# A dense and mixture-of-experts trunk on one core: other places for the adaLN weight sums in the mixer and in the dense channel mixer

## The chip, the cores and the metric

The kernel runs on one core of a Trainium2 chip. The metric is the device time of one execution in microseconds (us), given as the median of several runs. One profiled execution is read with the hardware profiler; its engines are TensorE (PE), VectorE (DVE), ScalarE (ACT), GpSimd (POOL) and SyncE (SP), which here issues most DMAs.

## What is computed

Two layers over 512 tokens of width 1024. Each layer has six modulation vectors (adaLN), each of 1024 numbers, that are a product of one row, silu(c), with a matrix of 1024 x 6144; a norm and a mixer (gated linear attention and retention); and a norm and a channel mixer, dense in layer 0, with 8 experts in layer 1.

```python
def reference(x, c, positions, ada_w, ada_b, norm_mix_g, norm_ffn_g, w_in, ...):
    cond = jax.nn.silu(c)
    for layer in range(DEPTH):                      # DEPTH = 2
        mod = (cond @ ada_w[layer] + ada_b[layer])[:, None, :]
        sh1, sc1, g1, sh2, sc2, g2 = jnp.split(mod, 6, axis=-1)
        h = rms_norm(x, norm_mix_g[layer]) * (1.0 + sc1) + sh1
        x = x + g1 * hybrid_mixer(h, positions, w_in[layer], ...)
        h = rms_norm(x, norm_ffn_g[layer]) * (1.0 + sc2) + sh2
        if layer % 2 == 0:
            y = swiglu(h, ffn_w1[i], ffn_w3[i], ffn_w2[i])     # D_FF = 2816
        else:
            y = moe_swiglu(h, router_w[i], moe_w1[i], moe_w3[i], moe_w2[i])
        x = x + g2 * y
    return rms_norm(x, final_g)
```

## The kernel before

The residual stream stays on the chip as eight tiles xT of 128 channels x 512 tokens. Weights arrive in f32 by SP's DMAs and are split into a high and a low f16 half: ACT casts hi (L202), DVE subtracts lo (L203). Each product of the mixers is three matmuls (mm3, L220 to L222): high x high, low x high, high x low.

**The adaLN sums.** The first two vectors of layer 0 are needed at once and have a path of their own. All others go through a queue of 40 units (ada_queue), in the order 2, 4, 3, 5 of layer 0 and then 1, 0, 2, 4, 3, 5 of layer 1; a vector has two column blocks q of 512, and a block has two units h, one for each half of the 1024 rows. ada_load issues the two DMAs of a unit (ada, 512 KB each) on POOL's queue into four buffers, so two units are in flight. ada_use adds its four row blocks into acc on DVE, each times a column of silu(c): the first by L297, the others by L299. After the second unit of a pair ACT casts the sum (acch, L305), DVE subtracts (accl, L306), and ada_sum is put on a list: eight one-column products on PE (pm, L232) that add over the partitions, and the modulation's columns on DVE (mod, L235). The list is emptied by ada_finish at the next call.

ada_some(n, least) makes n steps; a step uses the oldest unit if two have been loaded, and loads the next. With least = LATER = 28 it stops when 28 units are left in the queue, so that 12 units, the layer-0 vectors, belong to the layer-0 mixer and 28 to the dense channel mixer. ada_rest uses what has been loaded. Steps stand in the mixer at the end of each 256 columns of a projection (project) and in every second token tile of the value projections (project_v, n = 1 and 2); ada_rest stands after the first column block of the output projection. In the dense channel mixer (dense_ffn) ada_some(2) stands at the end of each of the 11 iterations of the up loop, which take 256 of the 2816 columns each, and after each of the four column blocks of the second products (pd); ada_rest stands at the end.

**The norms.** Norm.feed squares each new piece of xT (sq, L365, ACT) and adds the squares (ssq, L367, DVE). PE adds over the partitions (pms, L372), DVE takes the mean (ms, L379), computes the reciprocal root in steps (L340 to L347) and makes a diagonal (dg, L390) that PE spreads to all partitions (prb, L391); then DVE and ACT make the normed input in two halves (u, hl on DVE L406, L413; hh on ACT L408 to L412). The last column block of the output projection and of the second products is done in two halves of 256 tokens, and so is the norm behind it. Norm f is the one ahead of the dense channel mixer, norm m the one ahead of the second mixer; there PE also transposes xT to token-major tiles (tt, L1116), which ACT copies out (xt, L1118), before the first products pf_k and pf_q.

**What sets the order.** A scheduler puts the instructions of each engine in an order at build time; each engine then works its queue strictly in that order. The first sum of a unit keeps its place in program order (keep_in_program_order), and the pm products come after a product named by last_mm (issue_after). What depends on the emission order, such as where ada_some is called, so moves the order of all engines around it.

Of the kernel before, what the change touches and what calls it, by code (L numbers as in the profile page):

```python
# [117 lines left out]
def trunk(ctx, tc, a, out):  # L118
# [346 lines left out]
    def mixer(l, hh, hl, ws, sp, ga_bank=None, tokens=None):  # L465
# [18 lines left out]
        def project_v(c0, name):  # L484

            ws = [wsplit(w_in[:, i * 4:i * 4 + 4, c0:c0 + 512], 4, 512, f"{name}{l}_{i}") for i in range(2)]
            vs = []
            for t in range(NT):
                pt = psum(f"pv_{name}{l}_{t}", "pj")
                s = slice(t * P, (t + 1) * P)  # L490
                for k in range(KC):
                    wh, wl = ws[k // 4]
                    mm3(pt, hh[k][:, s], hl[k][:, s], wh[k % 4], wl[k % 4], k == 0, k == KC - 1)
                v = tl(f"{name}{t}", tag="v", bufs=5)
                nc.scalar.mul(v, pt, SCL)
                vs.append(v)
                if t % 2:
                    ada_some(t // 2 + 1, LATER)
            return vs


# [288 lines left out]
        w_out = kview(a["w_out"][l])  # L790
        if tokens:
            return tokens(tl, w_out, oh, ol)
        norm = Norm(f"f{l}")
        for c in range(0, D, 256):
            wh, wl = wsplit(w_out[:, :, c:c + 256], KC, 256, f"wo{l}_{c}")
            for half in (None,) if c < D - 256 else range(2):
                s = slice(0, T) if half is None else HALF[half]
                for b in range(2):
                    pj = psum(f"po_{l}_{c}_{b}_{half}", "pj")[:, 0:s.stop - s.start]
                    for k in range(KC):  # L800
                        mm3(pj, wh[k][:, b * P:(b + 1) * P], wl[k][:, b * P:(b + 1) * P], oh[k][:, s],
                            ol[k][:, s], k == 0, k == KC - 1)
                    d = c // P + b
                    nc.vector.scalar_tensor_tensor(
                        xT[d][:, s], pj, mods[l, 2][:, d:d + 1], xT[d][:, s], op0=ALU.mult, op1=ALU.add)
                    norm.feed(d, half)
            if c == 0:
                ada_rest()
        return norm


    def dense_ffn(hh, hl, sp, after):
# [3 lines left out]
        for f in range(0, nf, 2):  # L816
# [9 lines left out]
            for half, b in [(h, b) for h in range(2) for b in range(2)] if f == 0 else [(None, 0), (None, 1)]:  # L826
                s = slice(0, T) if half is None else HALF[half]
                pp, g = [x[:, s] for x in pps[b]], gs[b][:, s]
                steps = [(j, k) for j in range(2) for k in range(KC)]
                if half is not None:  # L830
                    steps.sort(key=lambda x: x[1])
                for j, k in steps:
                    c = slice(b * P, (b + 1) * P)
                    wh, wl = ((w1h, w1l), (w3h, w3l))[j]
                    mm3(pp[j], wh[k][:, c], wl[k][:, c], hh[k][:, s], hl[k][:, s], k == 0, k == KC - 1)
                nc.scalar.activation(g, pp[0], AF.Silu, scale=SCL)
                nc.vector.scalar_tensor_tensor(g, pp[1], 1.0 / WS, g, op0=ALU.mult, op1=ALU.mult)
                hi, lo = ah[f + b][:, s], al[f + b][:, s]
                nc.scalar.copy(hi, g)
                nc.vector.tensor_tensor(lo, g, hi, op=ALU.subtract)  # L840
            with behind(after if f < 4 else ()):
                ada_some(2)
        norm = Norm("m1")
        for c in range(0, D, 256):
# [3 lines left out]
            for half in (None,) if c < D - 256 else range(2):  # L848
# [7 lines left out]
                for b in range(2):  # L856
# [1 line left out]
                    nc.vector.scalar_tensor_tensor(  # L858
                        xT[d][:, s], pd[b], mods[0, 5][:, d:d + 1], xT[d][:, s], op0=ALU.mult, op1=ALU.add)
                    norm.feed(d, half)  # L860
            ada_some(2)
        ada_rest()
        return norm


# [646 lines left out]
```

## Time and profile before

| | us |
|---|---|
| median of 3 runs | 1400.43 (1398.14 to 1401.98) |
| the profiled execution | 1400.13 |
| its span, first to last instruction | 1398.4 |
| PE busy | 1335.8 |
| DVE busy | 1009.0 |
| ACT busy | 684.0 |
| granted clock of PE, mean | 0.968 |

The stages in the profiled execution: the first norm and loads up to about 70 us, the first mixer to 246, its output projection to 289, the up products of the dense channel mixer from 297 to about 525, its second products to 646, the second mixer from 664 to about 880, then the experts. The span is some 1.7 us shorter than the time of the same execution. Bars of busy time add up what an engine does, not what it waits for; a bracket at the end of a row of a timeline is the idle time ahead of it and what ended that.

### The profile page before, as it was taken

Reading aid. Unit: us, or ns where it says so; the run is one execution under the profiler, and the core shown is the slowest. Engines: PE = TensorE matmul, PEld = TensorE weight load, DVE = VectorE, ACT = ScalarE, POOL = GpSimd, SP = SyncE. Lnnn points to the kernel's source line nnn. Section 1 sums busy time; section 2 is a strip of 40 time slices with the busy share of each in tenths; the row PEclk is TensorE's granted clock in tenths of the full one; section 3 lists DMA queues with packets and bytes.
Section 4 is the critical chain, followed back from the end, with each engine's and each line's share of the span. In section 5 each row is a group of like instructions: output and inputs, shape, how many; then the busy total and the mean of one; then the engine's idle time right before and its main releaser. Section 6 shows DMA issues by size and latency. Waiting matters only on the chain.

```text
span 1398.4 us, 28543 instructions
## 1 busy us (share of the span) xinstructions
PE 1335.8 (96%) x11801; PEld 944.8 (68%) x11801; DVE 1009.0 (72%) x1849; ACT 684.0 (49%) x1099; POOL 167.5 (12%) x177
## 2 busy tenths in 40 slices
PE   6899999989999999997999999999999999999985
PEld 5455556475444444466755555579999999999983
DVE  6867887784676565656456876798988888878683
ACT  4362233443333323223552333477877877877563
POOL 0020100010111110110200310500000000000552
PEclk7789999989999999998999999999999999999997
DMA  9862452334565665453411210089999999989841
GB/s 325 291 210 92 132 170 64 121 120 144 197 230 174 201 212 173 152 205 104 138 61 61 91 36 1 1 316 384 356 323 348 360 315 361 352 303 353 310 154 63
DMA packets 167614, 279.79 MB, mean 200 GB/s; under 512 B 6352, under 2 KB 90332, under 8 KB 167476
## 3 DMA queue, kind: packets, MB, share of 16 engines
q1 hardware_dynamic: 153396, 229.01, 48.2%
q0 software_dynamic: 13936, 48.61, 10.5%
q8 instruction: 94, 1.54, 0.4%
q10 hardware_dynamic: 144, 0.26, 0.1%
q14 instruction: 44, 0.36, 0.1%
HBM read 271.80 MB, written 6.06 MB: 199 GB/s over the span
## 4 chain that ended last, share of the span: by engine, by line
PE 81%; DVE 9%; DMA 4%; ACT 3%; issue 1%; SPq 1%; POOL 0%; DVEq 0%; ACTq 0%; POOLq 0%
PE u L220 6%; PE u L221 6%; PE u L222 5%; PE eu L1153 5%; PE eu L1155 5%; PE eu L1152 5%; PE ed L1155 3%; PE ed L1153 3%; PE ed L1152 3%; PE pg L1174 2%; PE pd_None L220 2%; PE pd_None L222 2%; PE pd_None L221 2%; PE pj_gate L220 2%; PE pj_gate L221 2%; PE pj_gate L222 2%
## 5 line engine op out<-in xcount | busy, mean ns | idle before, releaser
L222 PE MATMUL u<-hh_f,lo_w 128*128 128x512 f16 (+1 forms) x384 | 139.7, 365 | 0.0
L221 PE MATMUL u<-hl_f,hi_w 128*128 128x512 f16 (+1 forms) x384 | 139.7, 365 | 0.0
L220 PE MATMUL u<-hh_f,hi_w 128*128 128x512 f16 (+1 forms) x384 | 138.2, 366 | 0.0
L203 DVE SCALAR_TENSOR_TENSOR lo_w<-raw_w,hi_w 128x512 f16<-128x512 f32 (+1 forms) x136 | 84.8, 674 | 52.1 <-ACT hi_w L202 52.0
L285 POOL DMA_DIRECT2D ada<-in_ada_w x80 | 57.9, 723 | 480.0 <-DVE acc L299 461.4
L202 ACT ACTIVATE hi_w<-raw_w 128x512 f16<-128x512 f32 (+1 forms) x136 | 72.8, 604 | 82.9 <-PE u L221 63.1
L299 DVE SCALAR_TENSOR_TENSOR acc<-ada,conds,acc 128x512 f32<-128x512 f32 x140 | 105.1, 750 | 3.5 <-DMA ada<-in_ada_w 0.7
L222 PEld LDWEIGHTS <-lo_w 128*128 128x128 f16 x604 | 59.6, 99 | 55.5
L220 PEld LDWEIGHTS <-hi_w 128*128 128x128 f16 x604 | 59.7, 99 | 54.1
L221 PEld LDWEIGHTS <-hi_w 128*128 128x128 f16 x604 | 59.5, 99 | 54.1
L1342 POOL DMA_INDIRECT y<-ybuf,rows x16 | 26.1, 1628 | 395.5 <-DMA raw_e7moe_w<-in_moe_w 388.7
L222 PE MATMUL pd_None<-ah,lo_w 128*128 128x512 f16 x132 | 50.1, 380 | 0.0
L221 PE MATMUL pd_None<-al,hi_w 128*128 128x512 f16 x132 | 50.1, 379 | 0.0
L220 PE MATMUL pd_None<-ah,hi_w 128*128 128x512 f16 x132 | 50.1, 379 | 0.0
L305 ACT CAST acch<-acc 128x512 f16<-128x512 f32 x20 | 12.3, 616 | 76.7 <-DVE acc L299 76.7
L220 PE MATMUL pj_gate<-hh_m,hi_gate 128*128 128x512 f16 x128 | 48.6, 379 | 0.8 <-ACT g L743 0.8
L222 PE MATMUL pj_gate<-hh_m,lo_gate 128*128 128x512 f16 x128 | 48.6, 380 | 0.0
L221 PE MATMUL pj_gate<-hl_m,hi_gate 128*128 128x512 f16 x128 | 48.6, 379 | 0.0
L203 DVE SCALAR_TENSOR_TENSOR lo_e7moe_w<-raw_e7moe_w,hi_e7moe_w 128x2048 f16<-128x2048 f32 (+3 forms) x21 | 39.1, 1872 | 7.7 <-ACT hi_e7moe_w L202 4.8
L203 DVE SCALAR_TENSOR_TENSOR lo_e5moe_w<-raw_e5moe_w,hi_e5moe_w 128x2048 f16<-128x2048 f32 (+1 forms) x18 | 37.9, 2112 | 8.8 <-ACT hi_e5moe_w L202 8.7
L203 DVE SCALAR_TENSOR_TENSOR lo_e2moe_w<-raw_e2moe_w,hi_e2moe_w 128x2048 f16<-128x2048 f32 (+1 forms) x18 | 38.0, 2113 | 7.4 <-ACT hi_e2moe_w L202 7.1
L203 DVE SCALAR_TENSOR_TENSOR lo_e3moe_w<-raw_e3moe_w,hi_e3moe_w 128x2048 f16<-128x2048 f32 (+1 forms) x18 | 37.9, 2111 | 6.6 <-ACT hi_e3moe_w L202 6.5
(570 smaller groups left out, 4187.8 us busy)
## 6 DMA issues: line engine op xcount, KB each, us to landing
ada<-in_ada_w POOLq DMA_DIRECT2D x80, 512.0 KB, 5.2
raw_w<-in_ffn_w SPq DMA_DIRECT2D x26, 1024.0 KB
raw_e1moe_w<-in_moe_w SPq DMA_DIRECT2D x12, 1024.0 KB
raw_e2moe_w<-in_moe_w SPq DMA_DIRECT2D x12, 1024.0 KB
raw_e3moe_w<-in_moe_w SPq DMA_DIRECT2D x12, 1024.0 KB
raw_e4moe_w<-in_moe_w SPq DMA_DIRECT2D x12, 1024.0 KB
raw_e5moe_w<-in_moe_w SPq DMA_DIRECT2D x12, 1024.0 KB
raw_e6moe_w<-in_moe_w SPq DMA_DIRECT2D x12, 1024.0 KB
```

The source lines that it names most:

```text
L202: nc.scalar.mul(hi, raw, WS)
L203: nc.vector.scalar_tensor_tensor(lo, raw, WS, hi, op0=ALU.mult, op1=ALU.subtract)
L220: nc.tensor.matmul(dst, wh, xh, start=first, stop=False)
L221: nc.tensor.matmul(dst, wh, xl, start=False, stop=False)
L222: last_mm[:] = [nc.tensor.matmul(dst, wl, xh, start=False, stop=last)]
L285: nc.gpsimd.dma_start(r, view[:, k:k + 2])
L299: op = nc.vector.scalar_tensor_tensor(acc, x, c, acc, op0=ALU.mult, op1=ALU.add)
L1152: nc.tensor.matmul(dst, wh[:, s], x1, start=(first and i == 0), stop=False)
L1153: nc.tensor.matmul(dst, wh[:, s], x2, start=False, stop=False)
L1155: nc.tensor.matmul(dst, wl[:, s], x1, start=False, stop=(last and i == len(ws) - 1))
L1174: nc.tensor.matmul(pg[:, 0:W], ht[j][t][d // 4][:, d % 4 * P:(d % 4 + 1) * P], oneh[:, t], start=(t == 0), stop=(t == NT - 1))
L1342: nc.gpsimd.indirect_dma_start(out=y, out_offset=None, in_=ybuf[half], in_offset=bass.IndirectOffsetOnAxis(ap=rows[:, i, t:t + 1], axis=0))
```

## The change

Three places at which sums are made are moved. In the value projections one step is made in each of the four token tiles (4 in all, 3 before). ada_rest stands ahead of the output projection. In the up loop one more step stands between the two halves of an iteration from the third iteration on (f from 4 on, where the tokens are not halved), and during the second products only ada_rest is left, after the first column block.

```diff
@@ project_v
-                if t % 2:
-                    ada_some(t // 2 + 1, LATER)
+                ada_some(1, LATER)
             return vs
@@ the mixer, ahead of the output projection
+        ada_rest()
         norm = Norm(f"f{l}")
         for c in range(0, D, 256):
@@ the output projection, end of a column block
-            if c == 0:
-                ada_rest()
@@ dense_ffn, up loop, end of a half b
                 nc.vector.tensor_tensor(lo, g, hi, op=ALU.subtract)
+                if half is None and b == 0:
+                    ada_some(1)
             with behind(after if f < 4 else ()):
                 ada_some(2)
@@ dense_ffn, second products, end of a column block
-            ada_some(2)
-        ada_rest()
+            if c == 0:
+                ada_rest()
         return norm
```

The three places in the order of the instructions. First DVE's queue at the end of the output projection, before. Here po_768_1_1 is the last product (last column block, second column tile, second token half), acc_3_1 the last pair of sums of layer 0, and ms_f_0 the mean of the first token half:

```order
420 L299 SCALAR_TENSOR_TENSOR acc_3_1_2296<-ada_3_1_4_2204,conds,acc_3_1_2296 128x512
421 L367 TENSOR_TENSOR ssq_f_2339<-ssq_f_2339,sq_f_None 128x512
422 L804 SCALAR_TENSOR_TENSOR xT_103<-po_768_0_1_2621,mod_2_670,xT_103 128x256
423 L299 SCALAR_TENSOR_TENSOR acc_3_1_2296<-ada_3_1_4_2204,conds,acc_3_1_2296 128x512
424 L367 TENSOR_TENSOR ssq_f_2339<-ssq_f_2339,sq_f_0_2568 128x256
425 L299 SCALAR_TENSOR_TENSOR acc_3_1_2296<-ada_3_1_6_2206,conds,acc_3_1_2296 128x512
426 L804 SCALAR_TENSOR_TENSOR xT_104<-po_768_1_1_2652,mod_2_670,xT_104 128x256
427 L299 SCALAR_TENSOR_TENSOR acc_3_1_2296<-ada_3_1_6_2206,conds,acc_3_1_2296 128x512
428 L306 TENSOR_TENSOR accl_3_1_2377<-acc_3_1_2296,acch_3_1_2376 128x512
429 L379 TENSOR_SCALAR ms_f_0_2603<-pms_f_0_2340 128x2
```

The same place after:

```order
412 L804 SCALAR_TENSOR_TENSOR xT_103<-po_768_0_0_2542,mod_2_670,xT_103 128x256
413 L804 SCALAR_TENSOR_TENSOR xT_104<-po_768_1_0_2573,mod_2_670,xT_104 128x256
414 L367 TENSOR_TENSOR ssq_f_2357<-ssq_f_2357,sq_f_0_2568 128x256
415 L804 SCALAR_TENSOR_TENSOR xT_103<-po_768_0_1_2621,mod_2_670,xT_103 128x256
416 L379 TENSOR_SCALAR ms_f_0_2603<-pms_f_0_2358 128x2
417 L340 TENSOR_SCALAR ry_f_0_2605<-ms_f_0_2603 128x2
```

The sums are gone from there (they stand before the first xT update of the projection), and the mean of the first half stands ahead of the last xT update. On PE the products pms_f of that mean stand, before, behind the last product of the projection and behind the first pm product; this is PE's queue before:

```order
2216 L222 LDWEIGHTS lo_wo_768_2533
2217 L222 MATMUL po_768_1_1_2652<-oh_3_0_2282,lo_wo_768_2533 128x256
2218 L232 LDWEIGHTS acch_3_1_2376
2219 L232 MATMUL pm_3_512_2380<-one_90,acch_3_1_2376 128x1
2220 L372 MATMUL pms_f_0_2340<-cst,ssq_f_2339 128x1 x2
2221 L372 MATMUL pms_f_0_2340<-cst,sq_f_0_2599 128x1 x2
2222 L232 LDWEIGHTS accl_3_1_2377
2223 L232 MATMUL pm_3_512_2380<-one_90,accl_3_1_2377 128x1
```

In the new order pms_f_0 stands behind the sixth of the 24 matmuls of po_768_1_1, and no pm product stands between that and the first u product. Second, PE's queue behind the second products: before, the transposes of the sixth tile of tt are separated from the fifth by the eight pm products of the last pair of layer 1 and by prb_m, the spread of the second half's norm:

```order
6094 L1116 MATMUL tt_0_5918<-cst,xT_103 128x128
6095 L1116 MATMUL tt_0_5918<-cst,xT_104 128x128
6096 L372 MATMUL pms_m_1_4901<-cst,sq_m_1_5697 128x1 x2
6097 L232 LDWEIGHTS acch_5_1_5720
6098 L232 MATMUL pm_5_512_5724<-one_90,acch_5_1_5720 128x1
6099 L391 MATMUL prb_m_1_5809<-dg_m_1_5808,cst 128x128 x2
6100 L232 LDWEIGHTS accl_5_1_5721
6101 L232 MATMUL pm_5_512_5724<-one_90,accl_5_1_5721 128x1
```

After:

```order
6118 L1116 MATMUL tt_2_5932<-cst,xT_103 128x128
6119 L1116 MATMUL tt_2_5932<-cst,xT_104 128x128
6120 L372 MATMUL pms_m_1_5028<-cst,sq_m_1_5730 128x1 x2
6121 L1116 MATMUL tt_3_5939<-cst,xT_101 128x128
6122 L1116 MATMUL tt_3_5939<-cst,xT_102 128x128
6123 L1116 MATMUL tt_3_5939<-cst,xT_103 128x128
6124 L1116 MATMUL tt_3_5939<-cst,xT_104 128x128
6125 L220 LDWEIGHTS hi_first_0_5738
6126 L220 MATMUL pf_k_0_6007<-hh_m_5777,hi_first_0_5738 128x256
```

No pm product is left there, the first products follow the transposes, and prb_m_1 stands behind 32 of them. On ACT all eight xt copies now stand ahead of the third hh. Third, the up loop on PE, after; before, the eight pm products of a pair stand between the last product of an iteration and the first of the next:

```order
3040 L222 LDWEIGHTS lo_w_6_3406
3041 L222 MATMUL u_6_0_3430<-hh_f_2697,lo_w_6_3406 128x512
3042 L232 LDWEIGHTS acch_5_1_3312
3043 L232 MATMUL pm_5_512_3372<-one_90,acch_5_1_3312 128x1
3044 L220 LDWEIGHTS hi_w_6_3405
3045 L220 MATMUL u_6_0_3430<-hh_f_2722,hi_w_6_3405 128x512
```

They now stand inside the products of one u tile.

## Rows read from the trace of the kernel before

**Rows 1.** Page, part 1: busy us (share of span) of each engine.

```profile
PE 1335.8 (96%) x11801; PEld 944.8 (68%) x11801; DVE 1009.0 (72%) x1849; ACT 684.0 (49%) x1099; POOL 167.5 (12%) x177
```

**Rows 2.** Busy time by stretches, columns as in the first line.

```profile
core 0: us, PE busy (x) PEld busy (x) DVE busy (x) ACT busy (x) POOL busy (x), PEclk, DMA share, GB/s
100.00:180.00 80.00, 80.00 (x434) 44.16 (x434) 63.89 (x161) 24.84 (x56) 4.44 (x7) 0.97 0.40 124
...
300.00:400.00 100.00, 100.00 (x563) 54.50 (x562) 62.65 (x110) 39.80 (x80) 12.56 (x17) 0.98 0.48 158
400.00:500.00 100.00, 100.00 (x500) 45.86 (x499) 67.97 (x110) 34.92 (x64) 14.46 (x20) 1.00 0.61 198
...
700.00:760.00 60.00, 60.00 (x328) 33.63 (x326) 39.17 (x98) 23.76 (x43) 0.00 (x0) 1.00 0.23 71
```

**Rows 3.** DVE, end of output projection: start, duration (us), engine, line, operation.

```profile
285.70 0.49 DVE L804 SCALAR_TENSOR_TENSOR xT<-po,mod,xT 128x256 f32<-128x256 f32 x1
...
288.41 0.43 DVE L367 TENSOR_TENSOR ssq_f<-ssq_f,sq_f 128x256 f32<-128x256 f32 x1
...
292.41 0.16 DVE L379 TENSOR_SCALAR ms_f<-pms_f 128x2 f32<-128x2 f32 x1 [0.44 <-PE pms_f L372]
...
294.22 0.48 DVE L390 TENSOR_SCALAR dg_f<-cst,ry_f 128x128 f32<-128x128 f32 x2
```

**Rows 4.** Timeline of PE, end of the output projection.

```profile
289.14 0.27 PE L222 MATMUL po<-oh,lo_wo 128*128 128x256 f16 x1
291.30 0.18 PE L232 MATMUL pm<-one,acch 128*128 128x1 f16 x1 [1.89 <-ACT acch L305]
291.34 0.58 PE L372 MATMUL pms_f<-cst,ssq_f 128*128 128x1 f32 x4
...
294.65 1.19 PE L391 MATMUL prb_f<-dg_f,cst 128*128 128x128 f32 x4 [2.11 <-DVE dg_f L390]
...
297.20 1.01 PE L220 MATMUL u<-hh_f,hi_w 128*128 128x256 f16 x4
```

**Rows 5.** Timeline of DVE behind the second products.

```profile
648.24 1.29 DVE L203 SCALAR_TENSOR_TENSOR lo_gv<-raw_gv,hi_gv 128x512 f16<-128x512 f32 x2
649.45 1.26 DVE L406 SCALAR_TENSOR_TENSOR u_m<-xT,A1m,prb_m 128x256 f32<-128x256 f32 x3
...
651.22 0.75 DVE L299 SCALAR_TENSOR_TENSOR acc<-ada,conds,acc 128x512 f32<-128x512 f32 x1
...
657.63 0.75 DVE L299 SCALAR_TENSOR_TENSOR acc<-ada,conds,acc 128x512 f32<-128x512 f32 x1
...
658.88 0.48 DVE L390 TENSOR_SCALAR dg_m<-cst,ry_m 128x128 f32<-128x128 f32 x2
```

**Rows 6.** Timeline of ACT behind the second products.

```profile
644.31 4.48 ACT L202 ACTIVATE hi_gv<-raw_gv 128x512 f16<-128x512 f32 x8 [1.15 <-PE pd L221]
...
660.99 1.55 ACT L1118 COPY xt<-tt 128x512 f32<-128x512 f32 x3
```

**Rows 7.** Timeline of PE behind the second products.

```profile
659.08 0.18 PE L232 MATMUL pm<-one,acch 128*128 128x1 f16 x1 [9.28 <-ACT acch L305]
...
664.44 0.42 PE L220 MATMUL pf_k<-hh_m,hi_first 128*128 128x256 f16 x1
```

**Rows 8.** Busy time by stretches around both places, columns as above.

```profile
292.00:296.00 4.00, 1.89 (x18) 1.83 (x17) 2.46 (x14) 0.00 (x0) 0.00 (x0) 0.60 0.57 194
296.00:300.00 4.00, 4.00 (x21) 3.19 (x21) 3.72 (x15) 1.76 (x4) 0.66 (x1) 0.50 0.00 0
660.00:664.00 4.00, 3.05 (x21) 2.84 (x20) 2.96 (x12) 3.62 (x9) 0.00 (x0) 0.50 0.00 0
```

**Rows 9.** Page, part 5 (L285, L299), and landing time of ada loads.

```profile
L285 POOL DMA_DIRECT2D ada<-in_ada_w x80 | 57.9, 723 | 480.0 <-DVE acc L299 461.4
...
L299 DVE SCALAR_TENSOR_TENSOR acc<-ada,conds,acc 128x512 f32<-128x512 f32 x140 | 105.1, 750 | 3.5 <-DMA ada<-in_ada_w 0.7
...
DMA to landing us min/median/max: 4.0/5.2/7.8
```

## The prediction

> **What bounds the kernel now.** First the busy line of the page: TensorE (PE) is busy for 1335.8 of 1398.4 us, so the time can only fall where PE stands still or where its clock is down [rows 1]. Then the busy time by stretches. In the mixer from 100 to 180 us and in the up products of the dense channel mixer from 300 to 500 us PE is busy all the time, VectorE (DVE) for 63 to 80% of it, and the DMA engines carry up to 198 GB/s [rows 2]. In such a stretch DVE work costs nothing as long as DVE keeps ahead. Third, the two places at which PE must wait for a norm, because everything that follows needs the whole residual stream: the end of the output projection (**A**, 285 to 298 us) and the end of the second products (**B**, 646 to 665 us). In both, adaLN sums stand in DVE's queue among the steps of the norm. At A the last product starts at 289.14, then PE waits 1.89 us for the cast of the adaLN sum (acch), and the first u product starts at 297.20 [rows 4]. At B PE waits 9.28 us for such a cast, up to 659.08, and the first pf_k product starts at 664.44 [rows 7]. The clock columns add a second price: around A the granted clock is 0.60, then 0.50, and from 660 to 664 us it is 0.50, while the undisturbed stretches show 0.98 to 1.00 [rows 8, 2]. A half clock is 1.2 instead of 2.4 GHz.
>
> **The change, part by part.** All 20 pairs of sums stay, each with eight DVE operations (0.75 us by the row, about 0.66 apart when back to back), one cast, one subtraction and eight one-column products [rows 9]. Nothing is removed; work moves.
>
> *A.* The eight sums of the last layer-0 pair leave the output projection. Before, the sum of squares of the first token half starts at 288.41 although its last input (xT at 285.70) ended at 286.2; the squaring on ScalarE I put at no more than 0.5 us, the price of an xt copy of twice the columns [rows 6], so two sums of 0.75 us (and a column of xT) delay it [rows 3]. PE has it worse: in its order one pm product, which waits for the cast, stands ahead of the mean (pms_f), and that one starts at 291.34. In the new order pms_f stands 18 products ahead of the end of the projection, with nothing of the adaLN before it. I follow it: xT done 286.2, square 286.7, sum of squares 287.1, pms_f 287.2 to 288.1 (it took 0.91 at 291.34), so ms_f at 288.3 in place of 292.41. The rsqrt chain from ms_f to dg_f took 1.81 us [rows 3], and one xT update of 0.5 comes in between: dg_f at 290.5, while the projection, 0.9 us later because of pms_f, ends at 290.2. From dg_f to prb_f 0.43, from there to the first u 2.55 [rows 4]: 293.5. So u starts 3.7 us earlier. Against it: the second half's square, sum and pms_f stand ahead of u on PE as before, and need xT of the last product, 290.7, plus 0.45, 0.45 and 0.9: 292.5, still in time. If the half clock, which lasts into the first u products, stays as long as before, the whole 3.7 is kept; I take **3.6**. Bounds: 2 (the chain is 1.5 us slower somewhere) and 6 (the clock does not fall, and the products of 297 to 302 us run at full speed).
>
> *B.* The last pair's eight sums, its cast, eight products and subtraction leave the tail. On DVE the seven operations of 0.75 us between 651.22 and 658.3, one of them after each step of the rsqrt chain, are gone (the first and the last of them in [rows 5]): 7 x 0.75 = 5.2 us, and the first one (0.48) before that. The chain of the second half's norm, which ended with dg_m at 658.88, then stands at about 654: two copies of weights' lower halves to 649.1, three u_m (1.26) to 650.3, two copies to 651.5, ms_m, seven steps of 0.2, and two hl_m of 0.6 in between: 654. On PE the eight pm products are gone, the remaining transposes tt follow at once, and prb_m goes behind the first 24 products. So the norm is no longer what PE waits for first; **what is late next is ScalarE**. Its queue ends the weight casts at 648.79 [rows 6]; after that in the new order two xt copies (0.52 each, 1.55 for three), one square of 0.4, three copies, and the first two hh_m (0.45 each): 648.8 + 1.0 + 0.4 + 1.55 + 0.45 = 652.2. That is where the first pf_k starts, in place of 664.44 [rows 7]. It does not run through from there: the PSUM buffers of the next pf_k and pf_q come free with the sixth to eighth xt copy, at 653.1 to 654.6, and the third hh_m stands behind them, at 655. Without waits the 24 products of the first two blocks take 24 x 0.109 = 2.6 us, so that a stream that runs through and ends them at the same time would have started at some 654.3 if the last third of them comes after the eighth copy. Gain 664.44 - 654.3 = 10.1 us at equal clock. But before, half speed held from 660 to 664 us at least, while PE still had transposes, so few of these products ran at it; now PE has long pauses from 650 to 652 and short ones up to 655, after which, as at A, the clock may fall for 8 us or so. At A it fell after a pause of about this size [rows 8]. Products of 3 us would then take twice their time: gain 7. I take **8.5**, nearer to the fallen clock; bounds 5 (the hh chain on ScalarE, some 1 us for each block, paces) and 10.5.
>
> *Where the sums go.* In the mixer, two more steps are taken in the value projections; each unit is summed a slot earlier, and eight sums of 0.66 to 0.75 come into the first steps of the linear attention: 63.89 + 6 = 70 of 80 us on DVE [rows 2]. In the up loop each iteration of 96 products at 0.2157 us, 20.7 us, gets a third unit: four sums and half a cast and a subtraction, 3.0 + 0.35 us. DVE goes from 68 of 100 to 84 of 100, and the DMA engines carry 1 MB more in 20.7 us, 198 + 50 = 248 GB/s [rows 2]. The loads are issued as soon as the sums free the buffers (POOL waits 461.4 us for them), and DVE waited 0.7 us in all for a load [rows 9]; the time between a load's issue and its use falls from some 20 to some 10 us against a landing time of 5.2, at most 7.8. The cover is PE's queue: u tiles of 5.2 us each in five PSUM buffers, some 10 us before DVE's lateness shows. I take **0**; bounds -1 (the sums that stood ahead of the decay's exponentials no longer do) and +3. No row shows DVE at 84% beside PE, hence the width.
>
> The POOL queue gets more loads in the up loop. What the trace shows is that every load landed within 7.8 us while DVE was 63 to 68% busy [rows 9, 2]. The Trainium skill, SBUF — State Buffer (SBUF: two separate sides), speaks against packing them there: a DMA issued by GpSimd cannot write its descriptors while DVE holds the shared port in a two-port operation, and its section on a bandwidth-pool intuition gives 620 ns alone against 3100 ns beside such an operation. Were all of the third unit's two loads late by that, an estimate from this page, 2 x 2.5 = 5 us an iteration, it would still lie within the 10 us that a load has.
>
> **Sum.** 3.6 + 8.5 + 0 = 12.1 us off the profiled execution's 1400.13 us: 1388.0. That execution lies 0.3 us under the median of 1400.43, so the same step from the median gives 1388.3; I say 1388. What comes after B shifts with it: in the next mixer PE is busy for 60.00 of 60 us [rows 2], so it keeps what it gets earlier.
>
> **Rivals.**
> - *Part of it is given back.* ScalarE's copies and hh_m pace B (gain 5), or the half clock lasts longer, or the fuller up loop costs up to 3: 2 + 5 - 0 to 3.6 + 8.5 - 3, gains of 4.3 to 9, 1391 to 1396. For it: ScalarE has eight copies of 0.52 and 12 operations of the norm in 12 us. Against it: PE's products need 12 us too.
> - *The clock stays up.* If the shorter pauses don't bring it down, A gives up to 6 and B up to 10.5: 14.5 to 16.5, 1383.6 to 1385.6. The rows speak against it: 0.50 after the pause at A [rows 8]. The Trainium skill, TensorE: Matmul & The Clock Gate (Part 1), has the throttled state as the default, which activity releases; by that rule, too, a pause that is merely shorter is not enough to be sure of the full clock.
> - *Slower.* In the new order the eight pm products stand inside the products of a u tile, not at a boundary between iterations, and PE takes its queue in order. If the cast of the sum isn't ready when PE comes to it, PE waits at each of the 14 pairs, with DVE at 84%. It decides from 12.1 / 14 = 0.87 us a pair; at the 1.89 us that the pm product waited at A [rows 4], 14 x 1.89 = 26.5, less 12.1: 14.4 us slower, 1414.5. Against it: no such wait in the stretches of 300 to 500 us now, PE 100.00 of 100 [rows 2], and about 3 us or more between sum and product in the new order.
> - *No change.* The same wait at about 0.6 to 1.1 us a pair, or a load that holds DVE's queue and with it the weights' lower halves: 1396 to 1404.
>
> **How the numbers follow.** Forecast (1386 to 1390.5) 54%; part given back 21%; clock stays up 11%; no change 7%; slower 7%. The range of 1383.5 to 1396.5 holds the first three, and leaves out the last two. Measurement of this kernel can tell some 0.3%, 4.2 us, from no change: the first three cases are faster than that, 0.86; within it 0.07; slower 0.07.
>
> **What would show it.** A: pms_f inside the last projection product, first u at about 293.5, no pm wait. B: no wait of PE for acch, first pf_k at about 652, ScalarE's xt copies as the releaser of what waits are left; clock 0.5 or so for some us around 655. Up loop: PE 100 of 100, DVE 80 to 85, DMA near 248 GB/s, no row of waits on acch. The prediction is wrong if PE waits for pm between 300 and 525 us, if the loads take over 10 us to land, or if pf_k starts later than 656.

## The result

The changed kernel took 1382.08 us (median of 4 runs, 1381.51 to 1383.10), the kernel before 1399.29 in the runs beside it; the ratio is 0.9882 with an interval of 0.9853 to 0.9910, some 16.5 us faster. A second set gave 1378.28 (1377.36 to 1386.05) and a ratio of 0.9891 (0.9853 to 0.9929). The forecast was 1388, with a range of 1383.5 to 1396.5: right in its direction and its places, too small in size, and the time lies 1.4 us below the range. One run of the kernel before, beside e1 to e5, took 5850.69 us and counts as a slow one; it is in no ratio, and nothing on record says why.

The profiled execution has a span of 1379.7 us against 1398.4. The busy line of its page answers to [rows 1]: PE has the same products, and 8.1 us less of busy time with a mean granted clock of 0.979 in place of 0.968.

```profile
PE 1327.7 (96%) x11801; PEld 939.7 (68%) x11801; DVE 1012.7 (73%) x1849; ACT 684.9 (50%) x1099; POOL 167.9 (12%) x177
```

The end of the output projection, PE's timeline after, answers to [rows 4]. Columns: start, duration, engine, line, operation, and in brackets the idle time before it.

```profile
290.21 0.27 PE L222 MATMUL po<-oh,lo_wo 128*128 128x256 f16 x1
291.25 0.71 PE L391 MATMUL prb_f<-dg_f,cst 128*128 128x128 f32 x4 [0.77 <-DVE dg_f L390]
291.87 0.58 PE L372 MATMUL pms_f<-cst,ssq_f 128*128 128x1 f32 x4
...
293.08 0.60 PE L220 MATMUL u<-hh_f,hi_w 128*128 128x256 f16 x4 [0.18 <-ACT hh_f L412]
```

The wait for the cast of the sum is gone; 0.77 us for the diagonal are left, and the first u product starts 2.87 us behind the last product of the projection, not 8.06.

Behind the second products, PE (answers to [rows 7]) and ACT (answers to [rows 6]):

```profile
645.62 0.50 PE L372 MATMUL pms_m<-cst,sq_m 128*128 128x1 f32 x4
645.98 0.63 PE L1116 MATMUL tt<-cst,xT 128*128 128x128 f32 x4
647.30 0.38 PE L220 MATMUL pf_k<-hh_m,hi_first 128*128 128x256 f16 x2 [0.68 <-ACT hh_m L412]
...
650.42 0.47 PE L391 MATMUL prb_m<-dg_m,cst 128*128 128x128 f32 x2
```

```profile
639.63 4.49 ACT L202 ACTIVATE hi_gv<-raw_gv 128x512 f16<-128x512 f32 x8 [1.14 <-PE pd L221]
644.02 1.05 ACT L1118 COPY xt<-tt 128x512 f32<-128x512 f32 x2
...
645.28 1.55 ACT L1118 COPY xt<-tt 128x512 f32<-128x512 f32 x3
646.70 0.94 ACT L412 ACTIVATE hh_m<-u_m,mod 128x256 f16<-128x256 f32 x2
...
648.39 1.10 ACT L1118 COPY xt<-tt 128x512 f32<-128x512 f32 x2
649.33 0.46 ACT L409 CAST hh_m<-u_m 128x256 f16<-128x256 f32 x1
```

One wait of 0.68 us is left of 9.28, and what ends it is ACT, as forecast. From there to the transposes of the gate PE has no wait of over 0.15 us.

Busy time by stretches, first those that answer to [rows 2], then those around the two places, [rows 8] (columns as there; the clock is the third number from the end):

```profile
300.00:400.00 100.00, 100.00 (x568) 52.98 (x566) 74.23 (x125) 40.03 (x79) 16.77 (x24) 1.00 0.63 200
400.00:500.00 100.00, 100.00 (x515) 46.09 (x514) 79.56 (x127) 34.48 (x63) 19.96 (x28) 1.00 0.76 250
...
100.00:180.00 80.00, 80.00 (x442) 43.18 (x441) 73.06 (x168) 23.39 (x50) 8.55 (x12) 0.98 0.52 163
```

```profile
292.00:296.00 4.00, 3.71 (x23) 2.77 (x24) 3.75 (x15) 1.75 (x4) 0.66 (x1) 0.71 0.00 0
296.00:300.00 4.00, 4.00 (x34) 3.36 (x33) 3.88 (x11) 3.05 (x8) 1.39 (x2) 0.86 0.00 0
...
644.00:648.00 4.00, 3.12 (x26) 2.43 (x25) 3.88 (x12) 4.00 (x11) 0.00 (x0) 1.00 0.87 270
648.00:652.00 4.00, 4.00 (x45) 3.64 (x44) 3.54 (x14) 3.66 (x10) 1.08 (x2) 1.00 0.74 258
```

In the up loop PE stays at 100.00 of 100 with DVE at 79.56 (forecast 84) and 250 GB/s (forecast 248). Behind the second products the clock stays at 1.00.

**Where the time went.** The starts of a few PE rows cut both executions into stretches; pv_gv are the products of the first value projection. The marks pxn and pc, in the experts, are starts of pieces of the chain of work that ended last, not the first rows of these names. The first two columns are the two profiles of the kernel before (the one shown and a second one, experiment f1), the last two those of the changed kernel (the one shown and experiment f2). All in us:

| stretch, from the start of a PE row to the next | before | before, f1 | after | after, f2 |
|---|---|---|---|---|
| start to the first pv_gv product | 73.62 | 70.62 | 72.20 | 70.19 |
| to the first product of the output projection | 172.71 | 169.39 | 174.39 | 174.39 |
| to the first u (A) | 50.87 | 51.23 | 46.49 | 46.49 |
| to the first u of 512 columns | 13.77 | 13.13 | 12.80 | 12.86 |
| to the first second product (up loop) | 219.48 | 219.49 | 220.29 | 220.29 |
| to the last second product | 115.95 | 115.95 | 115.55 | 115.56 |
| to the first pf_k (B) | 18.04 | 18.03 | 5.58 | 5.57 |
| to the transposes of the gate (pgt) | 15.91 | 17.25 | 16.62 | 16.63 |
| to the first piece of transposes of the experts' input on that chain (pxn) | 214.94 | 214.93 | 215.09 | 215.01 |
| to the first of the longer pieces of pc on that chain (final stage) | 467.23 | 468.11 | 465.85 | 464.65 |
| to the last of these pieces | 15.84 | 15.84 | 15.84 | 15.84 |
| to the end | 20.04 | 19.83 | 19.00 | 18.02 |

Between the two profiles shown, the stretches from pv_gv to pgt give +1.68 - 4.38 - 0.97 + 0.81 - 0.40 - 12.46 + 0.71 = -15.0 us. The other 3.7 of the 18.7 lie at the start, in the experts and at the end, where the change does nothing. The second pair gives less for the same stretches: +5.00 - 4.74 - 0.27 + 0.80 - 0.39 - 12.46 - 0.62 = -12.7 of 18.3 us. The changed kernel takes the same time in them in both profiles (591.7 and 591.8 us from pv_gv to pgt), the kernel before does not (606.7 and 604.5). Over all twelve profiles of this study the stretches outside take 785.6 to 791.6 us with the old end of the second products and 783.7 to 790.3 with the new one: the spread within each group is larger than the difference of the means, 1.7.

The stretch from pf_k to pgt is one of those that vary in the kernel before. Its granted clock, first in the profile shown, where pf_k starts at 664.44, then in f1, where it starts at 657.84:

```profile
664.00:668.00 4.00, 4.00 (x35) 3.49 (x34) 2.80 (x8) 4.00 (x12) 1.62 (x3) 0.89 0.03 7
```

```profile
656.00:660.00 4.00, 4.00 (x21) 3.33 (x20) 2.30 (x7) 4.00 (x12) 0.58 (x1) 0.50 0.00 0
660.00:664.00 4.00, 4.00 (x35) 3.50 (x33) 3.45 (x11) 3.72 (x11) 1.52 (x4) 0.87 0.03 7
```

The half clock behind the wait of 9.28 us reaches further into it in f1 (17.25 us) than in the profile shown (15.91); in the profile of experiment e1b it hardly reaches it, and the stretch takes 15.61.

### The profile page after: what moved, and what is told of

Same layout as the page of the kernel before. It is cut to its first block, busy times and chain, and to the rows that moved or that the text cites. A ratio compares the mean times of both kernels' runs of the same rounds, so it can differ in the third digit from the quotient of the medians.

```text
span 1379.7 us, 28545 instructions
## 1 busy us (share of the span) xinstructions
PE 1327.7 (96%) x11801; PEld 939.7 (68%) x11801; DVE 1012.7 (73%) x1849; ACT 684.9 (50%) x1099; POOL 167.9 (12%) x177
## 3 DMA queue, kind: packets, MB, share of 16 engines
q0 software_dynamic: 13936, 48.61, 10.8%
## 4 chain that ended last, share of the span: by engine, by line
PE 83%; DVE 6%; DMA 4%; ACT 2%; issue 1%; SPq 1%; POOL 1%; DVEq 0%; ACTq 0%; POOLq 0%
PE u L221 6%; PE u L222 6%; PE u L220 6%; PE eu L1152 5%; PE eu L1155 5%; PE eu L1153 5%; PE ed L1153 3%; PE ed L1152 3%; PE ed L1155 3%; PE pg L1174 2%; PE pd_None L221 2%; PE pd_None L222 2%; PE pd_None L220 2%; PE pj_gate L220 2%; PE pj_gate L221 2%; PE pj_gate L222 2%
## 5 line engine op out<-in xcount | busy, mean ns | idle before, releaser
L299 DVE SCALAR_TENSOR_TENSOR acc<-ada,conds,acc 128x512 f32<-128x512 f32 x140 | 104.9, 749 | 4.7 <-DMA ada<-in_ada_w 1.5
L285 POOL DMA_DIRECT2D ada<-in_ada_w x80 | 57.1, 714 | 347.7 <-DVE acc L299 331.6
L203 DVE SCALAR_TENSOR_TENSOR lo_e0moe_w<-raw_e0moe_w,hi_e0moe_w 128x512 f16<-128x512 f32 (+2 forms) x30 | 39.2, 1326 | 4.3 <-ACT hi_e0moe_w L202 4.1
```

The costliest lines, as they stand in the source:

```text
L203: nc.vector.scalar_tensor_tensor(lo, raw, WS, hi, op0=ALU.mult, op1=ALU.subtract)
L285: nc.gpsimd.dma_start(r, view[:, k:k + 2])
L299: op = nc.vector.scalar_tensor_tensor(acc, x, c, acc, op0=ALU.mult, op1=ALU.add)
```

## The experiments

**f1, f2: both kernels once more.** No edit.

> The kernel before once more, for a second profile. Theory 1 (the first profile of before, 1400.13, was a slow one of this kernel, by what happens at its ends): the stretches from the first pv_gv product to the first product of the output projection (172.7), from there to the first u (50.9), in the up loop (219.5), and from the end of the second products to the first pf_k (18.0) come out the same within 0.1, while the start, up to pv_gv, and the last 40 us differ by 1 to 2 us each, and the time lies at 1393 to 1399. Rival: the stretches themselves vary by more than 0.5.

> The changed kernel once more, for a larger sample on the same chip as the kernel before. Theory 1 (mixer +1.7, first u -4.4, clock behind it -0.6 to -2.2, up loop +0.8, second products -0.4, behind them -11.8): 14.7 to 16.3 us under the kernel before in the mean, ratio 0.988 to 0.990. Rival (the mixer part gains little or nothing on the whole, as its own run suggests): 11 to 13 us, ratio 0.9905 to 0.992.

The kernel before took 1393.86 us (median of 8), the changed one 1378.28 (median of 4). The table above shows what repeats: the stretches up to the first u (A), in the up loop and up to the first pf_k (B) come out within 0.4, most within 0.01. Those behind the first u and behind the first pf_k, where the clock is down in the kernel before, differ by 0.6 and 1.3. The start varies by 3 us, the last stretch by 2, and the experts by several: 464.65 to 468.33 over all profiles of this study. Against the expectation of f1 the mixer varied too: 169.39 in place of 172.71. Its granted clock tells why; the profile shown, with the wait ahead of it, and f1, the same instructions:

```profile
96.88 0.49 PE L573 MATMUL pbs<-cst,lge 128*128 128x128 f32 x2 [1.29 <-DVE lge L565]
```

```profile
96.00:100.00 4.00, 3.12 (x21) 3.12 (x21) 3.76 (x6) 3.97 (x8) 0.72 (x1) 0.78 0.20 30
100.00:104.00 4.00, 4.00 (x13) 1.96 (x13) 2.91 (x6) 2.12 (x5) 0.00 (x0) 0.50 0.89 289
```

```profile
96.00:100.00 4.00, 4.00 (x24) 2.15 (x23) 2.80 (x6) 3.99 (x9) 0.00 (x0) 1.00 0.81 229
100.00:104.00 4.00, 4.00 (x23) 1.81 (x23) 4.00 (x8) 1.67 (x4) 0.00 (x0) 1.00 0.49 168
```

Behind this wait of 1.29 us for the decay's logarithm (lge) the clock fell in three of four profiles with the old mixer, and in f1, with the same wait, it did not; between the two profiles that is worth 3.3 us. So a part of the spread of the kernel before (1391 to 1402 over its other runs) can be a clock that falls or not. The ratio of f2, 0.9891, is in the band of theory 1 (0.988 to 0.990), but its interval holds the rival too.

**e1: the mixer part alone.** The kernel before with

```diff
-                if t % 2:
-                    ada_some(t // 2 + 1, LATER)
+                ada_some(1, LATER)
...
+        ada_rest()
         norm = Norm(f"f{l}")
...
-            if c == 0:
-                ada_rest()
```

> The kernel before with the mixer part of the change alone: a step in each of the four token tiles of the value projections, and the rest of the sums ahead of the output projection. Theory 1 (what is gained lies at the two norms, and the two parts add): the first u product comes 4.4 us earlier counted from the first product of the output projection, and the first u tile of 512 columns 5.3 us earlier, the extra 1 us by the clock; the time falls by 5 us, and the end of the second products stays as it is (a wait of 9.3 us for acch at 659). Rival (part of the 17 us comes from the fuller steps, a different end of the experts or from run to run): the time falls by 3.6 us or less, or by more than 7.

1393.72 us (median of 10), ratio 0.9991 (0.9975 to 1.0007). In its profile the first u comes 46.49 behind the start of the projection, as in the changed kernel, and the first wide u another 11.19 behind that, with the clock at 1.00:

```profile
288.00:292.00 4.00, 3.23 (x28) 2.74 (x26) 3.23 (x14) 0.69 (x2) 0.00 (x0) 1.00 0.00 0
292.00:296.00 4.00, 3.71 (x33) 3.13 (x34) 3.75 (x17) 1.49 (x4) 0.67 (x1) 1.00 0.00 0
```

Its mixer took 174.41, 1.7 longer than 172.71, and the wait of 9.3 us at B is there. So A works as expected, but a part is given back in the mixer, which this expectation had left out: -4.4 and +1.7, and the clock behind A. What the runs show is less than that sum, and in the rival's range of 3.6 or less: the interval allows 3.5 us at most. The clock at lge is a part of the reason. From the first pv_gv product to the first u of 512 columns the old mixer takes 237.1 to 237.4 us in the three profiles in which the clock fell there, and 233.8 in f1, in which it did not; with the new order, in six profiles, it is 232.1 to 233.8. So the mixer part gains 3.3 us or more against the first three, and 0 to 1.7 against f1. By its runs it hardly pays.

**e1b: the steps alone**, without ada_rest being moved (the first hunk of e1 only).

> The kernel before with the steps in the value projections alone, without the rest of the sums being called ahead of the output projection. Theory 1 (it is the steps that empty the queue; the call that is moved finds nothing left): the first u comes 46.5 us behind the start of the output projection as with the whole mixer part, the mixer takes 174.4, and the wait of 9.3 us for acch behind the second products stays. Rival (the moved call does it): 50.9 and 172.7 as before.

A single run, 1393.80 us: 46.49 and 174.41, as in e1, and 18.04 at B. The steps empty the queue; in these stretches moving ada_rest does nothing more.

**e2: the channel-mixer part alone.**

```diff
+                if half is None and b == 0:
+                    ada_some(1)
             with behind(after if f < 4 else ()):
                 ada_some(2)
...
-            ada_some(2)
-        ada_rest()
+            if c == 0:
+                ada_rest()
```

> The kernel before with the channel-mixer part alone: a third step in the up loop, none in the second products but the rest. Theory 1: from the end of the second products to the first pf_k 5.6 us instead of 18.0, the clock stays at 1.00 there, the up loop costs 0.8 us more (four more sets of eight one-column products), so the time falls by 11 to 12 us; with the mixer part it adds up to some 17. Rival: the time falls by 8.5 (a clock that falls, or waits for the xt copies inside the first products), or the parts do not add.

1383.91 us (median of 4), ratio 0.9920 (0.9889 to 0.9950). The stretches are those of the changed kernel from the up loop on: 220.29, 115.55, 5.58 and 16.63; the mixer (172.69) and A (50.92) are those of before. -12.46 + 0.71 + 0.81 - 0.40 = -11.3 us by the stretches; 11.2 by the ratio. So B carries most of the gain. Whether the parts add the runs don't tell: by the ratios the two alone give 1.3 (e1) and 11.2, both together 15.2 and 16.5, and the intervals hold a plain sum.

**e3: something for PE to do in the wait at B.** The kernel before, with 36 products of 512 columns that nothing reads ahead of the last pm products:

```diff
+        if fill:
+            with tc.issue_after(fill[0].ins):
+                for _ in range(36):
+                    nc.tensor.matmul(pm, fill[1][:, 0:P], fill[1], start=True, stop=True)
...
```

Here fill[0] is the last product of the norm's mean (pms_m), and fill[1] a tile that is on the chip anyway.

> The kernel before, with 36 products of 512 columns (7.8 us) that nothing reads put into the wait of 9.3 us behind the second products; the sums stay there. The wait for acch is the same, only TensorE is not idle in it. Theory 1 (the clock is a second price of the wait): the granted clock stays near 1.00 from 652 to 668 us, the transposes and first products behind the wait run at full speed, and the time falls by 2 to 3.5 us. Rival (the wait alone is the price, and the work behind it is paced by VectorE and ScalarE): less than 1 us.

1398.48 us (median of 10), ratio 1.0011 (0.9995 to 1.0026): no gain. But the test does not settle what the clock is worth there. The filler ended at 656, two waits followed, and the clock fell all the same, a little later:

```profile
657.45 0.18 PE L237 MATMUL pm<-one,acch 128*128 128x1 f16 x1 [1.49 <-ACT acch L310]
660.33 0.37 PE L881 MATMUL pcols<-cst,cols 128*24 128x128 f32 x1 [1.13 <-DVE ones L1445]
```


```profile
652.00:656.00 4.00, 3.97 (x19) 1.58 (x17) 4.00 (x12) 0.00 (x0) 0.54 (x5) 1.00 0.80 270
656.00:660.00 4.00, 1.68 (x16) 1.21 (x16) 3.90 (x15) 2.55 (x6) 0.00 (x0) 0.93 0.00 0
660.00:664.00 4.00, 3.67 (x18) 3.15 (x19) 3.07 (x12) 4.00 (x12) 0.54 (x1) 0.50 0.02 4
```

From the last second product to pf_k it was 17.42 in place of 18.04, and from there to pgt 17.61 in place of 15.91 (17.25 in f1).

**e5: a longer pause at B in the changed kernel.** The first u_m is computed 11 times:

```diff
-            nc.vector.scalar_tensor_tensor(u, xT[k][:, s], A[:, k:k + 1], prb, op0=ALU.mult, op1=ALU.mult)
+            for _ in range(11 if self.name == 'm1' and k == 0 and half == 0 else 1):
+                nc.vector.scalar_tensor_tensor(u, xT[k][:, s], A[:, k:k + 1], prb, op0=ALU.mult, op1=ALU.mult)
```

> The changed kernel, with the first u_m behind the second products computed 11 times instead of once, 10 more operations of 0.42 us, some 4.0 to 4.2 us more on VectorE ahead of the rest of the norm. Against the changed kernel at 1382: theory 1 (a pause of some 3 us or more brings the clock down, one of 0.7 us does not): 4.2 us for the delay, and 1.5 to 3 for a half clock behind it, 1387.7 to 1389.3, with a granted clock of 0.5 to 0.8 somewhere between 648 and 660. Rival (only the delay counts): 1384 to 1386.3, clock at 1.00.

1387.07 us (median of 7), ratio 0.9947 to the kernel before. B is 9.89 instead of 5.58, and from there to pgt it takes 17.79 instead of 16.62: 4.31 for the delay and 1.17 behind it, 5.5 in all. The time lies between the ranges of theory 1 and the rival. PE's wait was 5.00 us, and this is what followed:

```profile
650.93 0.59 PE L220 MATMUL pf_k<-hh_m,hi_first 128*128 128x256 f16 x2 [5.00 <-ACT hh_m L413]
```


```profile
644.00:648.00 4.00, 1.93 (x16) 1.69 (x17) 4.00 (x14) 3.62 (x8) 0.00 (x0) 1.00 1.01 334
648.00:652.00 4.00, 1.07 (x6) 0.82 (x6) 4.00 (x15) 1.59 (x4) 0.00 (x0) 0.84 0.41 158
652.00:656.00 4.00, 4.00 (x31) 3.43 (x31) 4.00 (x11) 3.40 (x10) 2.42 (x4) 0.73 0.03 7
```

So, in the one profile of e5, the same place loses its clock when PE waits 5 us there; in all six profiles with a wait of 0.68 it keeps it. Where between the two it changes no run here tells, and the limit of some 3 us that the expectation names is not shown: at A the clock fell behind a wait of 0.77. The price, 1.2 us, is less than the 1.5 to 3 expected. PE was not waiting for DVE or ACT meanwhile (4.00 of 4.00 us busy from 652 to 656); by the windows' means the clock was back at some 654.

**e4: does the up loop cover more sums?** The changed kernel with two more operations in each unit of layer 1:

```diff
+            for _ in range(1 if l and i % 2 else 0):
+                nc.vector.scalar_tensor_tensor(acc, x, 0.0, acc, op0=ALU.mult, op1=ALU.add)
```

> The changed kernel with two more operations in each unit of the channel mixer's sums (x times 0 plus acc, which leaves acc as it is): some 2 x 0.66 us for each of 28 units, 4 us an iteration of 20.7, so VectorE goes from 80 to about 98 of 100 us in the up loop. Theory 1 (PE's queue and the PSUM buffers cover VectorE as long as it keeps up): PE stays at 100 of 100 and the time rises by less than 1.5 us. Rival (the products of the sums stand inside a u tile and hold PE when the cast is late): PE waits at pm in most of the 14 pairs, the time rises by 5 us or more.

1379.90 us (median of 4), ratio 0.9877 (0.9849 to 0.9905): no loss that the runs show (1378.28 in f2, on the same chip). The scheduler moved part of the sums into the second products (the last at 562 us), so DVE came to 86 and not to 98 of 100; PE waited for nothing in the loop:

```profile
300.00:400.00 100.00, 100.00 (x567) 52.97 (x565) 77.91 (x132) 39.46 (x79) 15.15 (x21) 1.00 0.59 185
400.00:500.00 100.00, 100.00 (x501) 45.86 (x499) 85.55 (x137) 34.40 (x63) 16.27 (x23) 1.00 0.71 224
```

The rival of waits at pm falls up to that load; what happens close to 100 was not reached.

**e7: the first value projection as before.**

```diff
-                ada_some(1, LATER)
+                if name == 'rv':
+                    ada_some(1, LATER)
+                elif t % 2:
+                    ada_some(t // 2 + 1, LATER)
```

> The changed kernel, with the first value projection's steps as before (in every second tile); only the second value projection takes a step in each tile. Theory 1 (the 1.7 us that the mixer got longer come from the two sums that stand in another order around the decay's exponentials and the first products of the attention): pv_gv to the output projection back from 174.4 to 172.7, the first u still 46.5 behind the start of the output projection, time 1.7 us under the changed kernel. Rival (the 1.7 us come from the second value projection or from the number of sums ahead of the output projection): 174.4 stays, or the first u comes later again.

1380.48 us (median of 4), ratio 0.9890. Each theory has one half: the mixer takes 171.66, less than the 172.7 of theory 1 and with the clock fallen behind the wait for lge as before, but the first u comes later again, 49.28 behind the start of the projection, so that both together take 220.94, against 220.88 in the changed kernel. The sums now stand right ahead of the projection, and its products wait for gate and output tiles there. PE's waits between 70 and 300 us, with what they were for, the total, the count and the longest:

```profile
PE po_None L220 <- ACT g L745: 2.0, 2, 1.3
PE pbs L575 <- DVE lge L567: 1.3, 1, 1.3
PE po_None L221 <- DVE ol L757: 1.1, 1, 1.1
```

**e8: no wait in front of the decay's products.** In the changed kernel PE waits 1.73 us for lge with 12 products of the first value projection still to do behind it:

```profile
95.47 0.59 PE L572 MATMUL pbs<-cst,lge 128*128 128x128 f32 x2 [1.73 <-DVE lge L564]
```

e8 puts them ahead of it:

```diff
+        gv = project_v(C_GV, "gv")
         la = [es[t // 2][:, (t % 2) * 256:(t % 2 + 1) * 256] for t in range(NT)]
...
             pbs = psum(f"pbs{l}_{p}")
-            for t in range(NT):
-                w = la[t][:, p * P:(p + 1) * P]
...
+            with tc.issue_after(last_mm[0].ins):
+                for t in range(NT):
+                    w = la[t][:, p * P:(p + 1) * P]
...
-        gv = project_v(C_GV, "gv")
```

> The changed kernel, with all products of the first value projection ahead of the products pbs that wait for the decay's logarithm (lge), so that TensorE has 12 products of 0.216 us (2.6 us) more to do while lge is made. Theory 1 (in the changed kernel's mixer a wait of 1.73 us for lge brings the clock to half for some 7 us, in all of its profiles, and in one of two of the kernel before): no wait at pbs, clock 1.00 from 88 to 108 us, and from the first pv_gv product to the output projection 169 to 171 us in place of 174.4; time 3.5 to 5 us under the changed kernel, 1374 to 1376. Rival (the 1.7 us that this stretch got longer are a matter of order, not of the clock): 1 to 2 us, 1377 or more.

1377.52 us (median of 4, 1375.12 to 1378.91), ratio 0.9875 (0.9850 to 0.9901). The wait is gone, the clock stays up, and the mixer takes 171.66 in place of 174.39. The changed kernel's stretches, then those of e8:

```profile
92.00:96.00 4.00, 2.27 (x17) 1.81 (x15) 0.96 (x2) 3.96 (x7) 0.00 (x0) 0.97 0.00 0
96.00:100.00 4.00, 4.00 (x21) 4.00 (x20) 2.54 (x5) 3.62 (x6) 0.00 (x0) 0.50 0.12 23
```

```profile
92.00:96.00 4.00, 4.00 (x30) 3.03 (x28) 2.87 (x6) 3.99 (x9) 0.71 (x1) 1.00 0.00 0
96.00:100.00 4.00, 4.00 (x28) 2.58 (x27) 4.00 (x7) 3.97 (x8) 0.71 (x1) 1.00 0.73 180
```

That is 2.7 us of the 3.5 to 5 expected: PE now waits 1.9 us more for gate tiles (g) further on. The changed kernel's wait, then that of e8 (total, count, longest):

```profile
PE pj_gate L220 <- ACT g L742: 0.8, 1, 0.8
```

```profile
PE pj_gate L220 <- ACT g L743: 2.7, 3, 1.1
```

The time itself lies in the rival's range (1377 or more). It has the lowest median of all versions here, but the runs alone don't tell it from the changed kernel.

## Why the prediction was right and wrong, by its own steps

- **What bounds the kernel, and what would be late next: right.** The waits for the cast are gone at both places, and at B what ends the wait that is left is ACT's chain of casts, copies and hh_m. The first pf_k was forecast 5.8 us behind the last second product (652.2 less 646.40) and came 5.58 behind it.
- **A: right in its mechanism, sized too small.** The first u was forecast 3.7 earlier; counted from the start of the projection it came 4.38 earlier. The clock was to cost as much as before, and cost less: from the first u to the first wide one 12.8 in place of 13.8 in the profiles shown, and 11.2 in two others with the same instructions. The chain was foreseen up to prb_f; what was too long is the 2.55 us from prb_f to the first u, read where the clock was at half. It took 1.83 with the clock at 1.00 (291.25 to 293.08). 3.6 forecast, 5.35 measured between the profiles shown and 5.01 between the second pair.
- **B: the step that failed.** 8.5 forecast, 12.46 - 0.71 = 11.75 measured between the profiles shown, and 11.4 to 13.1 with the other profiles of the old end. The start of pf_k was right; two deductions behind it were wrong. I took 2.1 us off because the next products would wait for the sixth to eighth copy of xt and the third hh_m. They didn't wait: no wait of over 0.15 us is left behind the first pf_k. The stretch to pgt grew all the same, by 0.7 between the profiles shown and by 1.0 against the one in e1b, which the half clock hardly reached. Most of that is work that has changed its place: prb_m and the transposes pcols stood ahead of the first pf_k before, and stand behind it now. And I took 1.6 off for a clock that falls. It stayed at 1.00, with one wait of 0.68 us in PE's way. I had PE pause from 650 to 652 with short gaps up to 655; the last transposes and the products of pms_m fill PE up to that 0.68 (645.62 to 646.6 in the rows above, which is 650.3 to 651.3 counted from the kernel before's last second product). In the profile of e5, with 5 us of waiting, the clock falls at this very place, and even then the stretch behind it takes only 1.2 more.
- **Moving the sums at no cost: wrong by 2.1 us, within the bounds of -1 to +3.** Against f1 it is 5.4, outside them. The up loop costs 0.81, since four more sets of eight one-column products stand in it (13 in place of 9; such a set takes 0.2 us), and the second products, with two sets fewer, give 0.40 of it back. The mixer takes 1.68 more than in the profile shown, and 5.00 more than in f1, where the clock stayed up. There the wait for lge is 1.73 in place of 1.29, and one more set of pm products comes in. With the wait of 1.73 the clock fell in all six profiles, and the stretch was 174.4 in each. e8 shows that 2.7 us are had back once PE has work in that wait; how the 1.68 divides is not settled.
- **The sum.** -5.35 + 2.1 - 11.75 = -15.0 between the profiles, 12.1 forecast. The second pair's 12.7 is nearer to that by luck: there the mixer part comes out at 0, and B at 13.1. Beyond that the profiles shown differ by 3.7 us in stretches that the change doesn't touch. Without these the time would have been some 1385, inside the range, so the 1.4 us below it are not the deductions at B alone. And the kernel before had been measured at 1400.43 in three runs where larger sets gave 1394.7 (22 runs) and 1396.2 (13). The forecast of a time hung on that first figure, too.
- **The rivals.** The one with the clock that stays up had the size of the result, 14.5 to 16.5, at a chance of 0.11; at B it held in every profile with the new end that was not delayed (six), at A in two of the eight that have its order there. The lower end of the rival that gives part of it back, 4.3, does not come out of its sum: 2 + 5 - 0 is 7, and with the 3 us of the up loop 4. The slower rival did not come: no wait at pm in the up loop, not at 86% of DVE either. I had also put down that loads of over 10 us would speak against me: of the sums' loads on POOL's queue none did. The longest took 8.2 us, in the up loop 7.5; 10.8 occurs among SP's loads of the first two vectors, issued in the first 30 us. DVE waited 1.5 us in all for loads, 0.7 before [rows 9].
- **The rule on the POOL queue.** In the up loop, with DVE at 80%, the loads landed in 4.1 to 7.5 us, 5.1 in the median; in the profile f1 of the kernel before it was 4.0 to 6.6, also 5.1 in the median. The 5.2 and 7.8 of [rows 9] rest on the 20 of the 80 loads whose landing that trace tells. The warning of the Trainium skill, SBUF — State Buffer (SBUF: two separate sides), about loads issued by GpSimd beside two-port operations is not borne out here as a price. No run here tells how long descriptors waited, nor how much of DVE's work here was two-port operations.

## What to carry to other kernels

Fillers that have slack, such as sums for a later layer, belong where the bounding engine has its densest work, and out of the few places at which it waits for the whole state; there even off-path operations of 0.75 us become the critical path, because they stand in the same queue. When a wait is taken away, count what is left of the pause before charging a fallen clock behind it, and give deductions for later waits only to what the engine really has no work for. Before a time is forecast, ask which of the reference runs are typical: many stretches between marked rows repeat to 0.01 us where totals differ by 6, and those that don't point to where a clock fell.

## What was not expected of the hardware

The granted clock can differ between executions of the same instructions. Behind A the clock stayed at 1.00 in two of the eight profiles with the changed order and fell in the others (0.71 and 0.59 from 292 to 296 us in the two of the changed kernel), at a price of 1.6 us (12.8 against 11.2); at the wait for lge it fell in three of four with the old mixer, at a price of 3.3 us (172.7 against 169.4). In both cases the wait ahead of it was short, 0.77 and 1.29 us. At B a wait of 0.68 us did not bring it down in six profiles. So the length of a wait alone does not tell what the clock will do. The Trainium skill, TensorE: Matmul & The Clock Gate (Part 1), says that the moment at which the clock rises varies from run to run. The rows agree: behind the wait of 9.28 us in the kernel before it was back by the time of the first pf_k in e1b, and some 3 us behind it in f1. They show besides that whether it falls at all can vary.
